# One-hot gate matrices in bf16, and the gate split into three bf16 parts

## The chip, the core and the metric

The program runs on one core of a Trainium2 chip. The metric is the device time of one execution in microseconds. The profile is one execution of the same program with the hardware profiler on; it names five engines: TensorE (PE for its matrix products, PEld for the weight loads ahead of them), VectorE (DVE), ScalarE (ACT), GpSimd (POOL) and the DMA queues issued by SyncE (SP).

## What is computed

The reference is a two-layer block (feed-forward, two kinds of attention), then a recurrent and an attention branch, and then a mixture of 16384 small experts (PEER). Only the last matters here. Each of the 256 tokens picks, for each of 8 heads, 16 experts out of 128 x 128 by two lists of 128 keys, and weighs them by a softmax:

```python
sc, ix = lax.top_k(s, PEER_TOPK)
cand = sc[:, :, 0, :, None] + sc[:, :, 1, None, :]
cidx = ix[:, :, 0, :, None] * PEER_N_KEYS + ix[:, :, 1, None, :]
top, pos = lax.top_k(cand.reshape(n, PEER_HEADS, PEER_TOPK * PEER_TOPK), PEER_TOPK)
eidx = jnp.take_along_axis(cidx.reshape(n, PEER_HEADS, -1), pos, axis=-1)
gate = jax.nn.softmax(top, axis=-1)
act = jax.nn.gelu(jnp.einsum('nhed,nd->nhe', expert_u[eidx], hb), approximate=False)
return jnp.einsum('nhe,nhed->nd', (gate * act).astype(hb.dtype), expert_v[eidx])
```

## The kernel before

The kernel does not gather experts. It computes the activation of all 16384 for all tokens, multiplies it by a gate that is zero for those that a token has not picked, and applies all of `expert_v`. An expert has two indices of 0 to 127; the first lies along the partitions, the second, i2, is the loop variable.

*u phases* (`u_phase`, 128 of them, one for each i2): 24 matrix products of 128 x 256 on TensorE, three for each of 8 slices, because fp32 weights are split in a high and a low fp32r part (`wblk`: a DMA brings 128 x 512 weights, ScalarE copies the high part, L200, and VectorE or GpSimd subtracts it for the low part, L206). ScalarE then writes the Gelu (L1299). Up to four such weight blocks are in flight.

*Scores and top-k* (`peer_scores`, `peer_topk`): ahead of them a norm (`norm`: for each of 8 slices ScalarE writes a high part L256 and a square L260, VectorE a low part L257) and the first queries, which ScalarE copies out as `qT`. Then a long chain on VectorE finds the picks. `res` holds, for each token, 128 picks (8 heads x 16): first index, second index, gate. While this runs, TensorE does the first 30 u phases.

*Gates* (`peer_gates`): `res` is transposed on TensorE so that the 128 picks lie along the partitions and the tokens along the row; five VectorE steps for each half of the tokens write them to `iT`: each index as a multiple of 8 and a remainder, and the gate.

*The stage of 64 gate groups* (`for tg in range(64)` in `peer`), four tokens each. For a token the gate matrix of 128 x 128 is a product over its 128 picks: a matrix with a one at each pick's first index, times a matrix with the gate at each pick's second index. `peer_hot` compares, for 16 tokens at a time, the multiple of 8 with 16 values and the remainder with 8 (L1441), and multiplies the gate into one of these (L1444). Every group then makes its two f32 matrices of 4 x 128 as products of a 16-wide and an 8-wide row (L1331, tiles `o0` and `o1`, two buffers each). TensorE multiplies them, one f32 product for each token (L1335, into a bank `pg`, two buffers). VectorE multiplies 30 columns of the result into activations that are already there (`ga0`, L1337), and ScalarE copies the other 98 to `ga1` (L1338). Between the groups lie 34 more u phases; all low parts L206 are VectorE's in this stage.

*v phases* (`v_phase`, L1355 to L1357) apply `expert_v`; in them the remaining 64 u phases. They reuse the tiles `o0` and `o1`. A linear stage (`ple`) ends the program.

A tile framework sets the order on each engine: it lists the instructions of every engine in a static order, found from the program's order and its own costs, and each engine then works its list strictly in that order, with semaphore waits between the engines.

Of the kernel before, what the change touches and what calls it, by code (L numbers as in the profile page):

```python
# [9 lines left out]
F32 = mybir.dt.float32  # L10
F32R = mybir.dt.float32r
I32 = mybir.dt.int32
U32 = mybir.dt.uint32
U16 = mybir.dt.uint16
BF16 = mybir.dt.bfloat16
AF = mybir.ActivationFunctionType
ALU = mybir.AluOpType
# [3 lines left out]
T = 256  # L21
# [1221 lines left out]
NKEY = 128  # L1243
# [24 lines left out]
class Prog3(Prog2):  # L1268
# [7 lines left out]
    def peer(self):  # L1276
        nc, tc, A = self.nc, self.tc, self.A
        E = ExitStack()
        with E:
            pp = E.enter_context(tc.tile_pool(name="pe", bufs=1))  # L1280
            C = {n: self.cload(pp, n) for n in ("ident", "iota")}
            ga0 = pp.tile([128, self.N0, T], F32, name="ga0")
            iT = pp.tile([128, 5, T], F32, name="iT")
            C["iota8"] = pp.tile([128, 16], F32, name="iota8")
            nc.vector.tensor_scalar(C["iota8"], C["iota"][:, 0:16], 8.0, None, op0=ALU.mult)
            ps = E.enter_context(tc.tile_pool(name="pps", bufs=2, space=PSUM))
            sp = E.enter_context(tc.tile_pool(name="psp", bufs=2))
            extra = {}

            def u_phase(i2):  # L1290
                if i2 < self.N0:
                    a = ga0[:, i2]
                elif self.N0 + self.NX <= i2 < self.N0 + self.NE:
                    a = extra[i2] = self.x[:, i2 - self.N0 - self.NX]
                else:
                    a = extra[i2] = sp.tile([128, T], F32, name="act", bufs=self.NX)
                p = ps.tile([128, 512], F32, name="pu")
                self.ws(p[:, :T], A["pu"][i2], self.xnh, self.xnl, KD)
                nc.scalar.activation(a, p[:, :T], AF.Gelu)  # L1299

            self.wsub = self.WS[0]
            tps = E.enter_context(tc.tile_pool(name="tps", bufs=2, space=PSUM))
            with tc.tile_pool(name="tk", bufs=1) as tk, tc.tile_pool(name="sps", bufs=4, space=PSUM) as sps:
                sc = self.peer_scores(tk, sps, ps)
                self.wsub = self.WS[1]
                res = tk.tile([128, 2, 3, HEADS_P, TOPK], F32, name="res")
                for t in range(2):
                    self.peer_topk(tk, sc[t], C, res[:, t])
                gates = self.peer_gates(tk, tps, res, iT, C)
                for i2 in range(self.N0):  # L1310
                    u_phase(i2)
                    if i2 in self.AT:
                        next(gates, None)
            ga1 = E.enter_context(tc.tile_pool(name="ga", bufs=1)).tile(
                [128, NKEY - self.N0, T], F32, name="ga1")
            xs = self.dram.tile([128, KD, T], F32, name="xp")
            nc.sync.dma_start(xs, self.x)
            self.wsub = self.WS[2]
            for tg in range(64):
                for i in range(tg * self.NE // 64, (tg + 1) * self.NE // 64):  # L1320
                    u_phase(self.N0 + i)
                pg = tps.tile([128, 4, NKEY], F32, name="pg")
                s = slice(tg * 4, tg * 4 + 4)
                if tg % 4 == 0:
                    hot = self.peer_hot(sp, iT, tg * 4, C)
                o = []
                for side in range(2):
                    o.append(sp.tile([128, 4, NKEY], F32, name=f"o{side}"))
                    u = slice(tg % 4 * 4, tg % 4 * 4 + 4)
                    B = [128, 4, 16, 8]  # L1330
                    nc.vector.tensor_mul(o[side].rearrange("p t (a b) -> p t a b", a=16),  # L1331
                                   hot[side][0][:, u, :, None].to_broadcast(B),
                                   hot[side][1][:, u, None, :].to_broadcast(B))
                for j in range(4):
                    nc.tensor.matmul(pg[:, j], o[0][:, j], o[1][:, j], start=True, stop=True)  # L1335
                a = ga0[:, :, s].rearrange("p i t -> p t i")
                nc.vector.tensor_mul(a, a, pg[:, :, :self.N0])  # L1337
                nc.scalar.activation(ga1[:, :, s].rearrange("p i t -> p t i"), pg[:, :, self.N0:], AF.Copy)  # L1338
            self.wsub = self.WS[3]
            vps = E.enter_context(tc.tile_pool(name="vps", bufs=1, space=PSUM))  # L1340
            acc = [vps.tile([128, 2, T], F32, name=f"acc{i}") for i in range(4)]

            def v_phase(i2, src):
                ph = sp.tile([128, 2 * T], F32R, name="o0")[:, 12:12 + T]
                pl = sp.tile([128, 2 * T], F32R, name="o1")[:, 12:12 + T]
                self.split(ph, pl, src)
                w = []
                for b in range(0, KD, self.wk):
                    w.append(self.wblk(A["pv"][i2][:, b * 128:(b + self.wk) * 128], self.wk * 128))
                for d in range(KD):  # L1350
                    o = acc[d // 2][:, d % 2]
                    vh, vl = w[d // self.wk]
                    s = slice(d % self.wk * 128, d % self.wk * 128 + 128)
                    first, last = i2 == 0 and d % 2 == 0, i2 == NKEY - 1
                    nc.tensor.matmul(o, vh[:, s], ph, start=first, stop=False, skip_group_check=True)  # L1355
                    nc.tensor.matmul(o, vh[:, s], pl, start=False, stop=False, skip_group_check=True)  # L1356
                    nc.tensor.matmul(o, vl[:, s], ph, start=False, stop=last, skip_group_check=True)  # L1357

            for i2 in range(NKEY):
                nx = i2 + self.N0 + self.NE  # L1360
                if i2 == NKEY // 2:
                    nc.sync.dma_start(self.x, xs)
                if nx < NKEY:
                    u_phase(nx)
                if i2 < self.N0:
                    v_phase(i2, ga0[:, i2])
                else:
                    g = ga1[:, i2 - self.N0]
                    nc.vector.tensor_mul(g, g, extra.pop(i2))
                    v_phase(i2, g)  # L1370
            self.wsub = "v"
            self.ple(sp, ps, tps, vps, acc)
# [55 lines left out]
        nc.vector.max(v[:, 8:16], tmp[:, :n])  # L1428
        nc.vector.max_index(i[:, 8:16], v[:, 8:16], tmp[:, :n])

    def peer_hot(self, sp, iT, t0, C):

        nc = self.nc
        s = slice(t0, t0 + 16)
        out = []
        for side in range(2):
            f = []
            for k, n in ((0, 16), (1, 8)):
                B = [128, 16, n]
                h = sp.tile(B, F32, name=f"h{side}{k}", bufs=1)  # L1440
                nc.vector.tensor_tensor(h, C["iota8" if k == 0 else "iota"][:, None, 0:n].to_broadcast(B),  # L1441
                                        iT[:, 2 * side + k, s, None].to_broadcast(B), op=ALU.is_equal)
                if side == 1 and k == 1:
                    nc.vector.tensor_mul(h, h, iT[:, 4, s, None].to_broadcast(B))  # L1444
                f.append(h)
            out.append(f)
        return out

    def peer_gates(self, tk, tps, res, iT, C):

        nc = self.nc
        B = [128, 2, HEADS_P, TOPK]
# [10 lines left out]
        for t in range(2):  # L1463
            pt = tps.tile([128, 4, NKEY], F32, name="pg")
            for j in range(3):
                nc.tensor.transpose(pt[:, j], res[:, t, j].rearrange("p h k -> p (h k)"), C["ident"])
            s = slice(t * 128, t * 128 + 128)
            ii = tk.tile([128, 2, NKEY], U32, name="ii")
            nc.vector.tensor_copy(ii, pt[:, 0:2])
            nc.vector.tensor_scalar(ii, ii, 7, None, op0=ALU.bitwise_and)  # L1470
            nc.vector.tensor_copy(iT[:, 1:4:2, s], ii)
            nc.vector.tensor_sub(iT[:, 0:4:2, s], pt[:, 0:2], iT[:, 1:4:2, s])
            nc.vector.tensor_copy(iT[:, 4, s], pt[:, 2])

    def peer_topk(self, tk, best, C, res):
        nc = self.nc
# [26 lines left out]
    def ple(self, sp, ps, tps, vps, acc):  # L1503

        nc, A = self.nc, self.A
# [6 lines left out]
        self.tmp, self.ps = Act, ps  # L1512
        pT = [Act.tile([128, T], F32, "p") for i in range(2)]
        ph = sp.tile([128, 2, T], F32R, name="o0")
        pl = sp.tile([128, 2, T], F32R, name="o1")
        for i in range(2):
            nc.sync.dma_start(pT[i], A["pT"][:, i])
            self.split(ph[:, i], pl[:, i], pT[i])
# [8 lines left out]
        for d in range(KD):  # L1527
            if d % 2 == 0:
                p = vps.tile([128, 2, T], F32, name=f"acc{d // 2}")
# [5 lines left out]
            s = Act.tile([128, T], F32, "s")  # L1535
# [56 lines left out]
```

## Time and profile before

| | us |
|---|---|
| three runs | 2194.35, 2195.75, 2196.25 |
| median | 2195.75 |
| the profiled execution | 2194.43 |
| its span, first to last instruction | 2192.6 |
| scores and top-k, about | 1300 to 1455 |
| the stage of 64 gate groups | 1460 to 1623 |
| v phases and the last stage | 1623 to 2192 |

The times of rows are microseconds from the start of the span. A row of the timeline has a start and a duration; instructions of an engine overlap, so what an engine can do in a stretch is read from start to start. Rows marked x3 or x16 are that many instructions in a row, and their duration runs from the first start to the last end.

### The profile page before, as it was taken

To read this page: it belongs to the slowest core of one execution; us is meant where nothing else is said; L and a number is where in the kernel's file an instruction comes from. 1 tells how busy PE (TensorE), PEld (TensorE's weight loads), DVE (VectorE), ACT (ScalarE), POOL (GpSimd) and SP (SyncE) were. 2 spreads that over 40 slices of the span, in tenths; PEclk is the share of its full clock that TensorE was granted. 3 is DMA by queue.
4 is the path that set the end of the run, shared out by engine and by line. 5 is a ranking of instruction groups with operands and counts; after the bars stand their busy time and mean duration, and the time that the engine had idled before them with its cause. 6 is when DMAs were issued, how large, how long until landed. Compare 5 with 4: busy or idle time off the path is not lost.

```text
span 2192.6 us, 48219 instructions
## 1 busy us (share of the span) xinstructions
PE 2092.4 (95%) x18034; PEld 2009.5 (92%) x18034; DVE 1602.2 (73%) x3315; ACT 1344.5 (61%) x2669; POOL 254.3 (12%) x250
## 2 busy tenths in 40 slices
PE   8999989999999999998897989889999999999997
PEld 8999779999999789998796789889999999999997
DVE  7766687767766677766995668999996666666666
ACT  6656676556656566657775656456665555555556
POOL 1001100000001100001210048950000000000000
PEclk9999999999999999999997999999999999999999
DMA  6666436666666336664353245543346666666663
GB/s 208 195 190 201 130 104 200 194 190 197 194 189 214 116 113 187 195 189 157 92 164 93 77 158 163 158 134 105 126 137 216 194 195 194 193 199 195 191 197 120
DMA packets 209659, 365.30 MB, mean 167 GB/s; under 512 B 31056, under 2 KB 39312, under 8 KB 208912
## 3 DMA queue, kind: packets, MB, share of 16 engines
q1 hardware_dynamic: 207312, 361.96, 54.7%
q8 instruction: 141, 2.31, 0.4%
q10 hardware_dynamic: 2112, 0.26, 0.1%
q14 instruction: 94, 0.77, 0.1%
HBM read 357.87 MB, written 4.26 MB: 165 GB/s over the span
## 4 chain that ended last, share of the span: by engine, by line
PE 75%; DVE 14%; ACT 4%; issue 4%; DMA 2%; POOL 1%; SPq 0%; DVEq 0%; ACTq 0%; POOLq 0%
PE mm L229 12%; PE mm L230 12%; PE mm L231 12%; PE acc L1357 5%; PE acc L1356 5%; PE acc L1355 5%; PE pu L230 4%; PE pu L229 4%; PE pu L231 4%; DVE wl L206 2%; PE pg L1335 2%; ACT wh L200 1%; DVE o L1331 1%; PE o L231 1%; PE o L229 1%
## 5 line engine op out<-in xcount | busy, mean ns | idle before, releaser
L200 ACT ACTIVATE wh<-wr 128x512 fp32r<-128x512 f32 (+1 forms) x1348 | 835.3, 624 | 618.7 <-PE mm L230 216.7
L206 DVE TENSOR_TENSOR wl<-wr,wh 128x512 fp32r<-128x512 f32 (+1 forms) x1256 | 866.6, 696 | 422.9 <-ACT wh L200 397.2
L229 PE MATMUL mm<-xn,wh 128*128 128x256 f32 x1840 | 512.4, 279 | 9.1 <-ACT wh L200 8.0
L231 PE MATMUL mm<-xn,wl 128*128 128x256 f32 x1840 | 509.8, 277 | 0.2 <-DVE wl L206 0.2
L230 PE MATMUL mm<-xn,wh 128*128 128x256 f32 x1840 | 509.9, 277 | 0.1
L229 PEld LDWEIGHTS mm<-xn,wh 128*128 128x128 f32 x1840 | 347.2, 189 | 12.0 <-ACT wh L200 9.5
L230 PEld LDWEIGHTS mm<-xn,wh 128*128 128x128 f32 x1840 | 347.2, 189 | 2.0 <-issue 1.2
L231 PEld LDWEIGHTS mm<-xn,wl 128*128 128x128 f32 x1840 | 346.9, 189 | 1.6 <-DVE wl L206 0.7
L231 PE MATMUL pu<-xn,wl 128*128 128x256 f32 x1024 | 283.8, 277 | 13.2 <-POOL wl L206 12.6
L229 PE MATMUL pu<-xn,wh 128*128 128x256 f32 x1024 | 285.9, 279 | 1.2 <-ACT ga L1299 1.2
L230 PE MATMUL pu<-xn,wh 128*128 128x256 f32 x1024 | 282.5, 276 | 0.0
L1355 PE MATMUL acc<-o,wh 128*128 128x256 f32 x1024 | 281.8, 275 | 0.6 <-ACT wh L200 0.6
L1357 PE MATMUL acc<-o,wl 128*128 128x256 f32 x1024 | 281.8, 275 | 0.2 <-DVE wl L206 0.2
L1356 PE MATMUL acc<-o,wh 128*128 128x256 f32 x1024 | 281.8, 275 | 0.0
L231 PEld LDWEIGHTS pu<-xn,wl 128*128 128x128 f32 x1024 | 192.4, 188 | 15.4 <-POOL wl L206 14.5
L229 PEld LDWEIGHTS pu<-xn,wh 128*128 128x128 f32 x1024 | 192.4, 188 | 1.4 <-ACT ga L1299 1.4
L231 PE MATMUL mm<-hh,wl 128*128 128x256 f32 x704 | 193.6, 275 | 0.0
L229 PE MATMUL mm<-hh,wh 128*128 128x256 f32 x704 | 193.6, 275 | 0.0
L230 PE MATMUL mm<-hh,wh 128*128 128x256 f32 x704 | 193.6, 275 | 0.0
L1355 PEld LDWEIGHTS acc<-o,wh 128*128 128x128 f32 x1024 | 192.3, 188 | 0.8 <-ACT wh L200 0.8
L1357 PEld LDWEIGHTS acc<-o,wl 128*128 128x128 f32 x1024 | 192.1, 188 | 0.4 <-DVE wl L206 0.4
L230 PEld LDWEIGHTS pu<-xn,wh 128*128 128x128 f32 x1024 | 192.4, 188 | 0.0
(444 smaller groups left out, 3741.0 us busy)
## 6 DMA issues: line engine op xcount, KB each, us to landing
wr<-in_ffn_gu SPq DMA_DIRECT2D x352, 256.0 KB, 3.0
wr<-in_pu SPq DMA_DIRECT2D x256, 256.0 KB, 2.9
wr<-in_pv SPq DMA_DIRECT2D x256, 256.0 KB, 2.9
wr<-in_ffn_d SPq DMA_DIRECT2D x160, 256.0 KB, 2.9
wr<-in_qk SPq DMA_DIRECT2D x64, 256.0 KB, 3.1
wr<-in_wo SPq DMA_DIRECT2D x48, 256.0 KB, 2.7
wr<-in_v SPq DMA_DIRECT2D x32, 256.0 KB, 2.9
wr<-in_u_g SPq DMA_DIRECT2D x32, 256.0 KB, 3.0
```

Of the source, the lines that this page charges most:

```text
L200: nc.scalar.activation(wh[:, :n], wr[:, :n], AF.Copy)
L206: (self.nc.gpsimd if eng == "p" else self.nc.vector).tensor_sub(out, a, b)
L229: self.nc.tensor.matmul(out, wh[:, s], h, start=first, stop=False, **kw)
L230: self.nc.tensor.matmul(out, wh[:, s], l, start=False, stop=False, **kw)
L231: self.nc.tensor.matmul(out, wl[:, s], h, start=False, stop=last, **kw)
L1331: nc.vector.tensor_mul(o[side].rearrange("p t (a b) -> p t a b", a=16), hot[side][0][:, u, :, None].to_broadcast(B), hot[side][1][:, u, No ...
L1335: nc.tensor.matmul(pg[:, j], o[0][:, j], o[1][:, j], start=True, stop=True)
L1355: nc.tensor.matmul(o, vh[:, s], ph, start=first, stop=False, skip_group_check=True)
L1356: nc.tensor.matmul(o, vh[:, s], pl, start=False, stop=False, skip_group_check=True)
L1357: nc.tensor.matmul(o, vl[:, s], ph, start=False, stop=last, skip_group_check=True)
```

## The change

The one-hot rows are no longer products of two short rows. An iota of 128 values, each repeated four times, is written in bf16 at the start (L1285, now a ScalarE copy; before, a VectorE step on 16 values). The two indices go to `iT` as they are, in bf16, which holds 0 to 127 exactly. The gate is written as three bf16 numbers whose sum is the fp32 gate: the gate in bf16, the rest in bf16, and the rest of that. A group then has two VectorE steps: one comparison of the iota with both indices of four tokens (L1325, 1024 elements), and one product of the second one-hot row with the three gate parts (L1328, 1536 elements). The four tokens of a group are innermost in these rows. TensorE does three bf16 products for each token, which add up in PSUM (L1332, 12 a group); it reads a token's columns four elements apart. Every bf16 product has a weight load of its own in the program. `peer_hot` is gone.

```diff
-            iT = pp.tile([128, 5, T], F32, name="iT")
-            C["iota8"] = pp.tile([128, 16], F32, name="iota8")
-            nc.vector.tensor_scalar(C["iota8"], C["iota"][:, 0:16], 8.0, None, op0=ALU.mult)
+            iT = pp.tile([128, 2, T], BF16, name="iT"), pp.tile([128, 3, T], BF16, name="gT")
+            C["iota4"] = pp.tile([128, NKEY + 8, 4], BF16, name="iota4")[:, :NKEY]
+            nc.scalar.activation(C["iota4"], C["iota"][:, :, None].to_broadcast([128, NKEY, 4]), AF.Copy)
...
-                if tg % 4 == 0:
-                    hot = self.peer_hot(sp, iT, tg * 4, C)
-                o = []
-                for side in range(2):
-                    o.append(sp.tile([128, 4, NKEY], F32, name=f"o{side}"))
-                    u = slice(tg % 4 * 4, tg % 4 * 4 + 4)
-                    B = [128, 4, 16, 8]
-                    nc.vector.tensor_mul(o[side].rearrange("p t (a b) -> p t a b", a=16),
-                                   hot[side][0][:, u, :, None].to_broadcast(B),
-                                   hot[side][1][:, u, None, :].to_broadcast(B))
+                one = sp.tile([128, 2, NKEY, 4], BF16, name="o0")
+                nc.vector.tensor_tensor(one, C["iota4"][:, None].to_broadcast([128, 2, NKEY, 4]),
+                                        iT[0][:, :, None, s].to_broadcast([128, 2, NKEY, 4]), op=ALU.is_equal)
+                og = sp.tile([128, 3, NKEY, 4], BF16, name="o1")
+                nc.vector.tensor_mul(og, one[:, 1:2].to_broadcast([128, 3, NKEY, 4]),
+                                     iT[1][:, :, None, s].to_broadcast([128, 3, NKEY, 4]))
                 for j in range(4):
-                    nc.tensor.matmul(pg[:, j], o[0][:, j], o[1][:, j], start=True, stop=True)
+                    for n in range(3):
+                        nc.tensor.matmul(pg[:, j], one[:, 0, :, j], og[:, n, :, j], start=n == 0, stop=n == 2)
...
-            ii = tk.tile([128, 2, NKEY], U32, name="ii")
-            nc.vector.tensor_copy(ii, pt[:, 0:2])
-            nc.vector.tensor_scalar(ii, ii, 7, None, op0=ALU.bitwise_and)
-            nc.vector.tensor_copy(iT[:, 1:4:2, s], ii)
-            nc.vector.tensor_sub(iT[:, 0:4:2, s], pt[:, 0:2], iT[:, 1:4:2, s])
-            nc.vector.tensor_copy(iT[:, 4, s], pt[:, 2])
+            nc.vector.tensor_copy(iT[0][:, :, s], pt[:, 0:2])
+            rest = tk.tile([128, NKEY], F32, name="rest")
+            nc.vector.tensor_copy(iT[1][:, 0, s], pt[:, 2])
+            nc.vector.tensor_sub(rest, pt[:, 2], iT[1][:, 0, s])
+            nc.vector.tensor_copy(iT[1][:, 1, s], rest)
+            nc.vector.tensor_sub(rest, rest, iT[1][:, 1, s])
+            nc.vector.tensor_copy(iT[1][:, 2, s], rest)
```

The change also makes the tile `o1` of the v phases and of the last stage half as large again, so that it has the size of the new matrix.

VectorE's list in the stage, a little after its start, before the change (`o` are the one-hot matrices, `h` the short rows, `ga` the scaling of activations, `wl` the low weight parts):

```order
L1331 TENSOR_TENSOR o_20225<-h_20218,h_20220 128x512
L1337 TENSOR_TENSOR ga_17787<-ga_17787,pg 128x4x30
L1331 TENSOR_TENSOR o_20273<-h_20214,h_20216 128x512
L1331 TENSOR_TENSOR o_20275<-h_20218,h_20220 128x512
L1337 TENSOR_TENSOR ga_17787<-ga_17787,pg 128x4x30
L1331 TENSOR_TENSOR o_20284<-h_20214,h_20216 128x512
L1331 TENSOR_TENSOR o_20286<-h_20218,h_20220 128x512
L206 TENSOR_TENSOR wl<-wr,wh 128x512 x3
L1337 TENSOR_TENSOR ga_17787<-ga_17787,pg 128x4x30
```

And the same list after it, at the same place (`iota` is the repeated iota, `gT` the gate parts):

```order
L1325 TENSOR_TENSOR o_20298<-iota_17790,iT 128x1024
L1334 TENSOR_TENSOR ga_17787<-ga_17787,pg 128x4x30
L1328 TENSOR_TENSOR o_20300<-o_20298,gT 128x1536
L1325 TENSOR_TENSOR o_20317<-iota_17790,iT 128x1024
L206 TENSOR_TENSOR wl<-wr,wh 128x512
L1328 TENSOR_TENSOR o_20319<-o_20317,gT 128x1536
L1334 TENSOR_TENSOR ga_17787<-ga_17787,pg 128x4x30
L1325 TENSOR_TENSOR o_20375<-iota_17790,iT 128x1024
L206 TENSOR_TENSOR wl<-wr,wh 128x512
L1334 TENSOR_TENSOR ga_17787<-ga_17787,pg 128x4x30
```

A group's two matrices L1331 have become L1325 and L1328, and the scaling (L1337, now L1334) still comes once a group, one or two matrices behind the one that it belongs to.

At the start of the expert part, VectorE's list of the norm loses the step that waits for the iota (`gh` are the norm's parts):

```order
 L324 TENSOR_TENSOR x<-k,o 128x256 x4
-L257 SCALAR_TENSOR_TENSOR gh<-x,vec,gh 128x256 x4
-L1285 TENSOR_SCALAR iota_17789<-c_iota 128x16
-L257 SCALAR_TENSOR_TENSOR gh<-x,vec,gh 128x256 x4
```

and ScalarE's list gains one, between its fourth and its fifth pair of the norm:

```order
 L256 ACTIVATE gh<-x,vec 128x256
 L260 ACTIVATE sq<-x 128x256
+L1285 ACTIVATE iota_17790<-c_iota 128x512
 L256 ACTIVATE gh<-x,vec 128x256
 L260 ACTIVATE sq<-x 128x256
```

So the wait for that DMA, which stood in the middle of VectorE's eight low parts, now stands in the middle of ScalarE's eight pairs.

## Rows read from the trace of the kernel before

**Rows 1.** The page, part 4: share of the span by engine.
```profile
PE 75%; DVE 14%; ACT 4%; issue 4%; DMA 2%; POOL 1%; SPq 0%; DVEq 0%; ACTq 0%; POOLq 0%
```

**Rows 2.** Busy time by windows: span, PE, PEld, DVE, ACT, POOL; clock, DMA share, GB/s.
```profile
1480.00:1600.00 120.00, 116.86 (x1003) 115.00 (x1002) 119.88 (x259) 75.62 (x126) 0.00 (x0) 1.00 0.35 114
...
sum 164.00, PE 159.05 PEld 156.14 DVE 161.41 ACT 102.54 POOL 0.00; mean PE 53.02 PEld 52.05 DVE 53.80 ACT 34.18 POOL 0.00
```

**Rows 3.** Groups by line, VectorE, 1455.5 to 1623: count, busy us, mean ns, idle before.
```profile
L1331 DVE TENSOR_TENSOR o<-h,h 128x512 f32<-128x512 f32 x128 | 83.2, 681 | 0.0
L206 DVE TENSOR_TENSOR wl<-wr,wh 128x512 fp32r<-128x512 f32 x72 | 46.4, 683 | 1.4 <-ACT wh L200 1.4
L1337 DVE TENSOR_TENSOR ga<-ga,pg 128x120 f32<-128x120 f32 x64 | 26.0, 406 | 0.3 <-PE pg L1335 0.2
L1441 DVE TENSOR_TENSOR h<-iota,iT 128x256 f32<-128x256 f32 x32 | 13.3, 415 | 0.0
L1441 DVE TENSOR_TENSOR h<-c_iota,iT 128x128 f32<-128x128 f32 x32 | 9.0, 282 | 0.0
L1444 DVE TENSOR_TENSOR h<-h,iT 128x128 f32<-128x128 f32 x16 | 4.5, 281 | 0.0
```

**Rows 4.** Timeline of VectorE in the stage: start us, duration us, instruction.
```profile
1499.97 0.41 DVE L1441 TENSOR_TENSOR h<-iota,iT 128x256 f32<-128x256 f32 x1
1500.31 0.28 DVE L1441 TENSOR_TENSOR h<-c_iota,iT 128x128 f32<-128x128 f32 x1
1500.51 0.41 DVE L1441 TENSOR_TENSOR h<-iota,iT 128x256 f32<-128x256 f32 x1
...
1501.85 0.40 DVE L1337 TENSOR_TENSOR ga<-ga,pg 128x120 f32<-128x120 f32 x1
1502.17 1.88 DVE L1331 TENSOR_TENSOR o<-h,h 128x512 f32<-128x512 f32 x3
```

**Rows 5.** Timeline of TensorE in the stage.
```profile
1502.59 0.28 PE L229 MATMUL pu<-xn,wh 128*128 128x256 f32 x1
...
1502.93 0.28 PE L229 MATMUL pu<-xn,wh 128*128 128x256 f32 x1
...
1503.84 1.87 PEld L1335 LDWEIGHTS pg<-o,o 128*128 128x128 f32 x16
```

**Rows 6.** Timeline of TensorE elsewhere: one-column products, and 64-column loads.
```profile
1249.62 1.15 PE L1211 MATMUL o<-k 128*64 128x64 f32 x32
...
1312.91 0.59 PE L276 MATMUL ps<-ones,sq 128*128 128x1 f32 x4
```

**Rows 7.** Timeline of VectorE from the gates to the last scaling.
```profile
1455.53 0.42 DVE L1469 CAST ii<-pg 128x256 uint32<-128x256 f32 x1 [0.42 <-PE pg L1466]
...
1458.97 0.28 DVE L1470 TENSOR_SCALAR ii<-ii 128x256 uint32<-128x256 uint32 x1
1459.17 0.28 DVE L1441 TENSOR_TENSOR h<-c_iota,iT 128x128 f32<-128x128 f32 x1
...
1460.64 0.68 DVE L1331 TENSOR_TENSOR o<-h,h 128x512 f32<-128x512 f32 x1
...
1622.40 0.42 DVE L1337 TENSOR_TENSOR ga<-ga,pg 128x120 f32<-128x120 f32 x1
```

**Rows 8.** Timeline of all engines in the norm ahead of the scores.
```profile
1300.90 0.42 SPq L170 DMA_DIRECT2D c_iota<-in_iota  x1
...
1303.30 0.49 ACT L256 ACTIVATE gh<-x,vec 128x256 fp32r<-128x256 f32 x1
...
1306.07 0.17 DVE L1285 TENSOR_SCALAR iota<-c_iota 128x16 f32<-128x16 f32 x1 [2.06 <-DMA c_iota<-in_iota]
...
1306.57 1.14 ACT L200 ACTIVATE wh<-wr 128x512 fp32r<-128x512 f32 x2
...
1310.40 0.66 ACT L1407 ACTIVATE qT<-pu 128x256 f32<-128x256 f32 x2 [2.70 <-PE pu L231]
```

More of the change, by code (lines that the diff above doesn't have):

```diff
@@ L1344, in v_phase @@
                 ph = sp.tile([128, 2 * T], F32R, name="o0")[:, 12:12 + T]
-                pl = sp.tile([128, 2 * T], F32R, name="o1")[:, 12:12 + T]
+                pl = sp.tile([128, 3 * T], F32R, name="o1")[:, 12:12 + T]
                 self.split(ph, pl, src)
@@ L1429, in top16 @@
         nc.vector.max_index(i[:, 8:16], v[:, 8:16], tmp[:, :n])
[L1431 to L1447, printed above, removed]
     def peer_gates(self, tk, tps, res, iT, C):
@@ L1514, in ple @@
         ph = sp.tile([128, 2, T], F32R, name="o0")
-        pl = sp.tile([128, 2, T], F32R, name="o1")
+        pl = sp.tile([128, 3, T], F32R, name="o1")
         for i in range(2):
```

## The prediction

> **What bounds the kernel now.** I read the page first: the chain that ended last is TensorE for 75% of the span [rows 1]. Outside one stage TensorE simply streams weights, and the change does not touch that. The stage it touches is the one in which u phases (24 products each) alternate with the 64 gate groups, so I cut the span there. In the 120 us from 1480 to 1600 TensorE shows 116.9 us busy and VectorE 119.9 us; in the whole stretch from 1460 to 1624 VectorE has 161.4 of 164 us [rows 2]. Both look full, so I counted each by starts. On VectorE, matrices of 512 elements follow one another every (1.88 - 0.68) / 2 = 0.60 us, those of 256 every 0.34, those of 128 every 0.20, and the scaling L1337 takes 0.32 from start to start [rows 4]: that is 0.07 us plus 1.04 ns for each element of a partition. On TensorE three u products take 1502.93 - 1502.59 = 0.34 us, 0.114 each, and the 16 halves of two gate groups follow one another every (1.87 - 0.19) / 15 = 0.112 us [rows 5].
>
> The sums by engine: VectorE, with the counts of [rows 3], 128 x 0.60 + 32 x 0.34 + 48 x 0.20 + 72 x 0.60 + 64 x 0.32 = 161.0 us, and 4.0 us for the ten small steps that turn the transposed gates into `iT` (1455.53 to 1460.64, less the four h matrices that lie among them), 165.0 in all. From the first of these steps to the end of the last L1337 there are 1622.40 + 0.32 - 1455.53 = 167.2 us [rows 7]. TensorE: 34 u phases x 24 x 0.114 = 93.0 and 512 x 0.112 = 57.3, 150 us. So VectorE bounds this stage with some 2 us of idle time, and TensorE has 11 us in hand. What comes after waits for the last L1337, and from there TensorE is the bound to the end; so what the stage gains or loses, the kernel gains or loses.
>
> **The gate matrices, on VectorE.** Out go the two 512-wide products of a group and the 20 h steps of every 16 tokens: 128 x 0.60 + 32 x 0.34 + 48 x 0.20 = 97.3 us. In come, for each of 64 groups, a comparison of 1024 bf16 elements (L1325) and a product of 1536 (L1328). No VectorE row here has bf16 on two sides. One end is one element at a time, as in [rows 4]: 0.07 + 1.04 x 1.024 = 1.13 and 0.07 + 1.04 x 1.536 = 1.67 us. The other end is cost by bytes: 1024 bf16 elements are the 2048 bytes of a 512-wide f32 matrix, 0.60 us, and 1536 are 0.07 + 1.04 x 0.768 = 0.87. A one-source step on 256 uint32 elements moved on after 0.20 us where two-source ones need 0.34 [rows 4, 7], so the engine can take two at a time in some form. I take the lower end: rows of four adjacent tokens leave every operand with neighbours innermost, which is what the layout is for. Then 64 x (0.60 + 0.87) = 94.1 us, a gain of 3.2. With the upper ends it would be 179.2, a loss of 82.
>
> The Trainium skill's page "VectorE: DVE Perf Modes", section "The perf-mode tier table", says that a two-source step on bf16 in SBUF runs at twice the fp32 rate; by it the sum is the same 94.1 us, and no run here shows it yet.
>
> **The splitting of the gate, on VectorE.** Ten steps at 4.0 us become twelve: two of 256 elements and ten of 128, 2 x 0.34 + 10 x 0.20 = 2.7 us, and some 0.1 us more at each of four places where a step needs the one ahead of it: 3.1. A gain of 0.9. These stand ahead of the first matrices, on the chain.
>
> **The gate products, on TensorE.** A group's 4 f32 products (8 halves, 0.90 us) become 12 bf16 ones, each with its own weight load. The trace has no bf16 product, so I bound a load with its product. A 128-column f32 load costs 0.113 us even if the product behind it has a single column ((0.59 - 0.25) / 3) [rows 6]: the load alone sets that pace. Loads of 64 f32 columns with 64-column products come every (1.15 - 0.22) / 31 = 0.030 us, two side by side, so 0.06 for one [rows 6]; a 128-column bf16 load has as many bytes. So a group costs between 12 x 0.06 = 0.72 and 12 x 0.112 = 1.34 us. With the lower end, to which I hold because both operands are half as wide, TensorE needs 93.0 + 46 = 139 us, well under VectorE, and the change of this term brings nothing: VectorE still ends last. The two engines meet where 93.0 + 768x = 157, at x = 0.083 us.
>
> Here a rule of the Trainium skill speaks against me and another for me. "TensorE: Matmul & The Clock Gate", section "LDWEIGHTS (loading the stationary operand)", gives a load as its columns over 1.2 GHz and names no type: 107 ns for 128 columns, an estimate by that page, which would make the stage as long as the first rival does. The f32 row of 0.113 agrees with it. The same page's section "Weight-path perf modes" says that loads of 128 columns that are not fp32 are read several elements at a time, which would give the lower end; no row here shows it.
>
> **What is queued where.** In VectorE's queue L1334, the scaling that waits for a group's products, stands right behind the next group's matrix, or one L206 behind it, as L1337 did. With 0.72 us for the products that wait is over before its turn, as now (0.3 us lost in the whole stage) [rows 3]. With 1.34 it is not, and L206 and the next matrices behind it wait too.
>
> **The iota, at the start of this part.** Before, VectorE waited 2.06 us at L1285 for the iota to land (issued 1300.90, there by 1306.07), and four low parts of the norm stood behind it [rows 8]. Now ScalarE waits there, after its fourth norm pair. Its fifth pair began at 1303.30; it will begin at 1306.07 plus 0.55 for a copy of 512 elements. Four pairs at (1306.57 - 1303.30) / 4 = 0.82 and the two weight copies (1.14) bring the two qT copies to 1306.62 + 3.28 + 1.14 = 1311.0 in place of 1310.40 [rows 8]. That is 0.6 us later, and VectorE's long top-k chain behind it starts as much later. Its ends: 0, if the iota lands sooner, and 3, if the two weight copies (3.3 us later than now) are waited for.
>
> **Sum.** -3.2 - 0.9 + 0.6, and -0.5 for VectorE's 1.4 us idle at the end of the stage, where TensorE, now lighter, was late [rows 3] (its ends 0 and -1.4): -4.0 us. The profiled execution took 2194.43 us and becomes 2190.4; the median of the runs shown is 2195.75, 1.3 higher, so I say **2191.8 us**. A kernel of this length tells no change from one under 0.2%, 4.4 us, which puts the edge at 2191.4: the forecast lies just inside "same". Its own range is 2188 to 2196, from 0.03 us on either bf16 step (64 x 0.06 = 3.8).
>
> **Rivals.**
> - *The weight load sets the pace of TensorE.* For it: the one-column row [rows 6]. Against it: half the bytes. Then a group's 12 products take 1.34 us, the stage's TensorE work is 93.0 + 768 x 0.112 = 179 us against the 161.8 us that this stretch has now (1460.64 to 1622.4) [rows 7], and VectorE stalls in L1334: slower by 17 to 21 us, 2213 to 2217. It decides from x = 0.083; from there to 0.1 it gives 2193 to 2207.
> - *VectorE takes the bf16 elements one at a time.* For it: every two-source row of the trace does [rows 4]; operands are repeated across the row with a step of nothing. Against it: the innermost run of four. Price 64 x (2.80 - 1.47) = 85 us, about 2277; if only the comparison falls back, 64 x 0.53 = 34, about 2226.
> - *The bf16 steps cost less than by bytes*, by 0.05 us or more each, or the idle time at both ends goes: 64 x 0.1 = 6 us more, about 2185. TensorE's 139 us leave room for it.
>
> **Chances.** Forecast 0.55, nearly half of it under the edge; full load pace 0.20 and the stretch between 0.10 (four parts in ten of it same); one at a time 0.10; cheaper steps 0.05. Faster by over 0.2%: 0.26 + 0.05 = 0.31. Same: 0.29 + 0.04 = 0.33. Slower: 0.20 + 0.06 + 0.10 = 0.36. The range, 2187 to 2217, takes in the load pace and leaves out the one-at-a-time rival, the end of the load pace and most of the cheap steps, under 0.2.
>
> **What will show it.** L1325 near 0.68 us and L1328 near 0.95 in their own durations (0.08 above start to start), against 1.2 and 1.75; the gate products' starts 0.06 apart, against 0.11; VectorE at over 97% of the stage with TensorE's share falling under 90%; no time lost ahead of L1334; ScalarE's 2.7 us wait at L1285 and qT copies at 1311. I am wrong if TensorE, not VectorE, is full from 1480 to 1600, or if a stage without gate work changes its length.

## The result and the profile after

The changed kernel takes 2214.8 us, the median of four runs (2212.5 to 2223.7), against 2195.05 for the four runs of the kernel before that are compared with it (2193.2 to 2196.3): 1.010 times the time, 95% interval 1.0086 to 1.0114. It is some 20 us slower. The profiled execution of the changed kernel took 2223.66 us, 9 over its median; a second trace of the same kernel, taken later, has a span of 2215.0 us, against 2192.6 before. The two agree in all that follows except where it is said.

The stage of 64 gate groups is where the time went. From the first gate step to the end of the last scaling it takes 1649.67 + 0.42 - 1456.13 = 194.0 us (192.6 in the second trace), where the same reckoning gives 167.3 before [rows 7]. What lies after the stage takes 571.7 us (569.5) in place of 569.8, and the stage begins 0.6 us later (2.6 us earlier) than before.

The page, part 4, the chain that ended last, by engine (before: [rows 1]):

```profile
PE 80%; DVE 10%; ACT 4%; issue 3%; DMA 2%; POOL 1%; SPq 0%; DVEq 0%; ACTq 0%; POOLq 0%
```

Busy time in the stage by windows: span, PE, PEld, DVE, ACT, POOL; clock, DMA share, GB/s (before: [rows 2]):

```profile
1480.00:1600.00 120.00, 120.00 (x1022) 117.43 (x1020) 102.22 (x166) 67.69 (x106) 0.00 (x0) 1.00 0.29 93
```

The two engines have changed places. TensorE is busy for all of the 120 us, with 1022 products: 0.117 us each. VectorE, which was the bound, is idle for 18 of them.

VectorE's groups by line in the whole stage (before: [rows 3]); the last number is the idle time ahead of them:

```profile
L1328 DVE TENSOR_TENSOR o<-o,gT 128x1536 bf16<-128x1536 bf16 x64 | 60.3, 952 | 0.0
L206 DVE TENSOR_TENSOR wl<-wr,wh 128x512 fp32r<-128x512 f32 x72 | 49.0, 685 | 1.6 <-ACT wh L200 1.4
L1325 DVE TENSOR_TENSOR o<-iota,iT 128x1024 bf16<-128x1024 bf16 x64 | 43.2, 685 | 0.0
L1334 DVE TENSOR_TENSOR ga<-ga,pg 128x120 f32<-128x120 f32 x64 | 26.7, 417 | 25.9 <-PE pg L1332 25.3
```

Nearly all of VectorE's 28 us of idle time stands in one place: 25.9 us ahead of the scaling L1334, 25.3 of it for the gate products. Before, the same step waited 0.3 us.

A piece of VectorE's timeline, and TensorE's gate products in the same 7 us (start, duration, instruction; the bracket is idle time and what ended it; before: [rows 4, 5]):

```profile
1518.61 0.68 DVE L1325 TENSOR_TENSOR o<-iota,iT 128x1024 bf16<-128x1024 bf16 x1
1519.83 0.42 DVE L1334 TENSOR_TENSOR ga<-ga,pg 128x120 f32<-128x120 f32 x1 [0.54 <-PE pg L1332]
1520.16 0.95 DVE L1328 TENSOR_TENSOR o<-o,gT 128x1536 bf16<-128x1536 bf16 x1
1521.03 0.69 DVE L1325 TENSOR_TENSOR o<-iota,iT 128x1024 bf16<-128x1024 bf16 x1
...
1516.67 1.58 PE L1332 MATMUL pg<-o,o 128*128 128x128 bf16 x12
1518.21 1.58 PE L1332 MATMUL pg<-o,o 128*128 128x128 bf16 x12
```

L1328 starts 1521.03 - 1520.16 = 0.87 us ahead of the next step, and L1334 0.33: VectorE's own prices are those of the forecast. But a group's twelve products take 1.58 us. Since one of them lasts 0.30, they start (1.58 - 0.30) / 11 = 0.116 apart, where the forecast had 0.06. The question for the runs was what holds a bf16 product of 128 columns at 0.117 us.

### The profile page after: what moved, and what is told of

It is laid out like the page before. It is cut to its first block, busy times and chain, and to the rows that moved or that the text cites. A ratio compares the mean times of both kernels' runs of the same rounds, so it can differ in the third digit from the quotient of the medians.

```text
span 2221.8 us, 48590 instructions
## 1 busy us (share of the span) xinstructions
PE 2127.2 (96%) x18290; PEld 2044.2 (92%) x18290; DVE 1604.7 (72%) x3236; ACT 1350.9 (61%) x2670; POOL 253.4 (11%) x250
## 4 chain that ended last, share of the span: by engine, by line
PE 80%; DVE 10%; ACT 4%; issue 3%; DMA 2%; POOL 1%; SPq 0%; DVEq 0%; ACTq 0%; POOLq 0%
PE mm L230 12%; PE mm L229 12%; PE mm L231 12%; PE acc L1354 5%; PE acc L1353 5%; PE acc L1352 5%; PE pu L229 5%; PE pu L230 5%; PE pu L231 5%; PE pg L1332 4%; DVE wl L206 1%; ACT wh L200 1%; PE o L231 1%; PE o L229 1%; PE o L230 1%
## 5 line engine op out<-in xcount | busy, mean ns | idle before, releaser
L200 ACT ACTIVATE wh<-wr 128x512 fp32r<-128x512 f32 (+1 forms) x1348 | 837.2, 625 | 636.4 <-PE mm L230 219.9
L229 PE MATMUL mm<-xn,wh 128*128 128x256 f32 x1840 | 512.6, 279 | 9.4 <-ACT wh L200 8.4
L229 PEld LDWEIGHTS mm<-xn,wh 128*128 128x128 f32 x1840 | 347.5, 189 | 12.1 <-ACT wh L200 9.8
L229 PE MATMUL pu<-xn,wh 128*128 128x256 f32 x1024 | 287.0, 280 | 0.7 <-ACT ga L1299 0.7
L229 PEld LDWEIGHTS pu<-xn,wh 128*128 128x128 f32 x1024 | 194.4, 190 | 1.0 <-ACT ga L1299 0.9
L229 PE MATMUL mm<-hh,wh 128*128 128x256 f32 x704 | 193.6, 275 | 0.0
```

The lines of the kernel that those rows point to most:

```text
L200: nc.scalar.activation(wh[:, :n], wr[:, :n], AF.Copy)
L229: self.nc.tensor.matmul(out, wh[:, s], h, start=first, stop=False, **kw)
```

## Experiments

All run times stand beside runs of the kernel before on the same chip: 2192.6 us (13 runs) for neighbouring columns on both sides, half of the moving columns, one product and one token innermost; 2194.2 (13 runs) for neighbouring columns on one side and two tokens innermost; 2193.5 (11 runs) for the place of the tiles. "Stage" is the time from the first gate step to the end of the last scaling.

### Neighbouring columns on both sides

```diff
-nc.tensor.matmul(pg[:, j], one[:, 0, :, j], og[:, n, :, j], ...)
+f = lambda x: x.rearrange("p k t -> p (k t)")[:, j * 128:j * 128 + 128]
+nc.tensor.matmul(pg[:, j], f(one[:, 0]), f(og[:, n]), ...)
```

> Each of the 768 gate products reads 128 neighbouring bf16 columns of the two matrices, for the weights and for the moving side, in place of columns four elements apart. Number and size of loads and products stay; the gate values are wrong, since the columns of four tokens are mixed. Theory A, the step of four elements in the rows makes load or product slow: starts of the products fall from 0.117 us to about 0.06, the stage is VectorE's again and the kernel takes about 2190 us. Theory B, a bf16 load of 128 columns costs what an f32 one does, whatever its layout: starts stay at 0.112 to 0.117, TensorE is full, and the time stays at 2210 to 2218 us.

Measured: 2186.4 us (one run), 0.056 us from product to product, a stage of 161.8 us. Since it mixes the columns of four tokens, this kernel is a probe and not one to use. Number, type and size of loads and products are unchanged, so neither the count of 768 loads nor "a load costs what it costs" explains the loss. The step of four elements does. With it gone, this run is 6 us under the median before, and the forecast's picture of the stage holds.

### Which side: weights or moving columns

One run gives only the weight loads neighbouring columns, another only the moving side.

```diff
+flat_weights: nc.tensor.matmul(pg[:, j], f(one[:, 0]), og[:, n, :, j], ...)
+flat_moving:  nc.tensor.matmul(pg[:, j], one[:, 0, :, j], f(og[:, n]), ...)
```

> Only the weight loads read 128 neighbouring columns; the moving side keeps its step of four elements. The gate values are wrong, since weights of four tokens are mixed. After the runs with both sides neighbouring (0.056 us from start to start, 2186.4 us) the step is the cause; this run and the next tell which side. Theory A1, the moving columns: starts stay at 0.117 us, TensorE stays full, 2210 to 2218 us. Theory A2, the weight columns: 0.056 us and about 2187 us.

> Only the moving side reads 128 neighbouring columns; the weight loads keep their step of four elements. The gate values are wrong in the same way. Theory A1, the moving columns: 0.056 us from start to start and about 2187 us; the run with 64 moving columns, 0.061 us, speaks for it. Theory A2, the weight columns: 0.117 us and 2210 to 2218 us.

A gate group on TensorE with neighbouring weights, from the timeline:

```profile
1502.81 1.55 PE L1332 MATMUL pg<-o,o 128*128 128x128 bf16 x12
```

And with neighbouring moving columns, with its twelve loads:

```profile
1501.11 0.86 PE L1332 MATMUL pg<-o,o 128*128 128x128 bf16 x12
...
1501.11 0.71 PEld L1332 LDWEIGHTS <-o 128*128 128x128 bf16 x12 [0.17 <-DVE o L1328]
```

With neighbouring weights alone, nothing is won: 2220.5 us (one run), stage 191.2. With neighbouring moving columns alone, all of it is: 2190.0 us (one run), stage 162.0, products (0.86 - 0.22) / 11 = 0.058 us apart, and the loads, still with their step of four elements, keep up. So it is the moving side. A 128-column bf16 load takes 0.058 us or less even with the step; a 128-column moving side with that step takes 0.117.

VectorE's and TensorE's busy time from 1480 to 1600 with neighbouring moving columns (columns as above):

```profile
1480.00:1600.00 120.00, 116.58 (x1237) 110.22 (x1234) 120.00 (x202) 81.67 (x130) 0.00 (x0) 1.00 0.36 114
```

VectorE is full again, and TensorE does 1237 products where it did 1022.

### Half of the moving columns

```diff
+h = 64 if n else 128
-nc.tensor.matmul(pg[:, j], one[:, 0, :, j], og[:, n, :, j], ...)
+nc.tensor.matmul(pg[:, j, :h], one[:, 0, :, j], og[:, n, :h, j], ...)
```

> The second and third product of each token move 64 columns in place of 128; loads as in the changed kernel. It leaves half of the columns of two gate parts out. Theory B, the load sets the pace: starts stay at 0.112 to 0.117 us and the time at 2210 to 2218. Theory C, the moving columns set it: 512 of the 768 products come after 0.06 us, TensorE's work falls by 512 x 0.057 = 29 us and the kernel takes about 2190 us.

A gate group on TensorE (the form in the row is that of its first product; eight of the twelve move 64 columns):

```profile
1501.93 1.15 PE L1333 MATMUL pg<-o,o 128*128 128x128 bf16 x12 [0.18 <-DVE o L1328]
```

The product behind one of 64 moving columns starts 0.060 to 0.063 us after it, the one behind one of 128 columns 0.119: the cost goes with the moving columns, 0.93 to 0.98 ns each at this step. Theory C was right on the product and wrong on the time: 2206.4 us (one run), stage 179.0. The mean of one product is here (0.119 + 2 x 0.062) / 3 = 0.081 us. The stage holds 36 u phases, as is told below, so TensorE's sum is 36 x 24 x 0.114 + 768 x 0.081 = 161 us. VectorE's is as much, 64 x (0.60 + 0.87 + 0.32) + 72 x 0.60 = 157.8 us and 3 for the splitting of the gate. But VectorE still lost 13.2 us ahead of the scaling (L1335 here), nearly all of it waiting for the products (L1333), and TensorE 5.0 waiting for the matrices:

```profile
L1335 DVE TENSOR_TENSOR ga<-ga,pg 128x120 f32<-128x120 f32 x64 | 26.8, 418 | 13.2 <-PE pg L1333 12.6
...
L1333 PE MATMUL pg<-o,o 128*128 128x64 bf16 (+1 forms) x768 | 72.6, 260 | 5.8 <-DVE o L1328 5.0 <-ACT wh L200 0.7
```

With about the same amount of work on both, handed over in a fixed order, neither engine was full in this run: each waited for the other in turn.

### One product in place of three

```diff
-for n in range(3):
+for n in range(1):
```

> VectorE's work is that of the changed kernel, but TensorE does only the first of the three products of a token: 256 loads and products in place of 768. It leaves the two smaller gate parts out of the sum. Whatever makes a product slow, TensorE then has 36 u phases x 24 x 0.114 + 256 x 0.117 = 128 us against VectorE's 161, so VectorE must bound the stage: the forecast for VectorE alone is 2190 to 2192 us, 4 us less than before, and L1334 waits for nothing. If the stage stays near 194 us, it was not the number of gate products that made it longer.

Measured: 2194.9 us (10 runs, 2187.9 to 2201.3), 1.0006 times before, interval 0.9993 to 1.002; stage 166.2 us. The number of products is thus what made the stage longer, but the 4 us that were expected beside it are not in the median. The trace is of a run of 2199.9 us. It is late already where the norm ahead of the scores begins, at 1303.3 us in place of 1300.5 before, and what comes after the stage takes 572.7 us in place of 569.8; the stage itself is 1.1 us shorter than before. In the stage the scaling waited 4.6 us for the products, and TensorE, idle for 16 of the 166 us, was not at its full clock throughout: the granted clock from 1560 to 1600 was 0.96 and 0.95, in the runs with neighbouring columns 1.00.

```profile
1560.00:1580.00 20.00, 17.04 (x124) 14.13 (x124) 18.68 (x32) 12.50 (x22) 0.00 (x0) 0.96 0.38 115
1580.00:1600.00 20.00, 18.69 (x139) 16.39 (x139) 18.95 (x33) 12.03 (x20) 0.00 (x0) 0.95 0.36 107
```

The two fastest of the ten runs, at 2187.9 us, have a mean granted clock of 0.990 over the span, the others 0.983 to 0.985. That the clock makes the spread is likely by this, not shown: there is one trace, and it is of one of the longest.

### One token innermost

The 128 keys stand innermost in the rows, so that TensorE reads neighbouring columns, and VectorE reads an index or a gate part as one value that is repeated along the row.

```diff
-one = sp.tile([128, 2, NKEY, 4], BF16, name="o0")
+one = sp.tile([128, 2, 4, NKEY], BF16, name="o0")
-iT[0][:, :, None, s].to_broadcast([128, 2, NKEY, 4])
+iT[0][:, :, s, None].to_broadcast([128, 2, 4, NKEY])
```

(and the same for `og`, with the iota no longer repeated)

> The same three bf16 products, with the 128 keys innermost in the rows in place of the four tokens; nothing is left out. TensorE reads neighbouring columns, and in both VectorE steps the index or gate part is one value repeated along the row. Theory A: starts near 0.06 us. Theory B: 0.112 to 0.117. On VectorE, if what made 1024 and 1536 elements cost 0.60 and 0.87 us is that the innermost run holds four different neighbours on every operand, they cost 1.13 and 1.67 now, VectorE has 64 x (1.13 + 1.67) + 64 = 243 us in the stage and the kernel takes about 2270 us. If a repeated value does no harm, VectorE is as in the changed kernel, and by A the time is about 2190 us, by B 2210 to 2218.

VectorE's groups by line between 1456 and 1650 (columns as above):

```profile
L1328 DVE TENSOR_TENSOR o<-o,gT 128x1536 bf16<-128x1536 bf16 x50 | 86.1, 1756 | 0.0
L1325 DVE TENSOR_TENSOR o<-iota,iT 128x1024 bf16<-128x1024 bf16 x50 | 59.4, 1221 | 0.0
```

From start to start they take 1.13 and 1.67 us, the one-element prices of the forecast's second rival. A piece of VectorE's timeline has one of each:

```profile
1518.58 1.22 DVE L1325 TENSOR_TENSOR o<-iota,iT 128x1024 bf16<-128x1024 bf16 x1
1519.72 0.69 DVE L206 TENSOR_TENSOR wl<-wr,wh 128x512 fp32r<-128x512 f32 x1
1520.32 1.76 DVE L1328 TENSOR_TENSOR o<-o,gT 128x1536 bf16<-128x1536 bf16 x1
1521.99 0.69 DVE L206 TENSOR_TENSOR wl<-wr,wh 128x512 fp32r<-128x512 f32 x1
```

TensorE's products are 0.056 us apart, and it doesn't help: 2294.5 us (two runs), stage 248.9. So the four tokens innermost are what lets VectorE take two bf16 elements at a time, and the same layout is what halves TensorE's moving side. The Trainium skill's page "Vector Engine (DVE) Microarchitecture Reference", section "Performance modes — why throughput varies by op and dtype", says that one element read over and over as an operand of a two-source bf16 step keeps the step at one result a cycle; the two steps above, at 1.13 and 1.67 us, agree.

### Two tokens innermost

```diff
-one = sp.tile([128, 2, NKEY, 4], BF16, name="o0")
+one = sp.tile([128, 4, NKEY, 2], BF16, name="o0")
-og = sp.tile([128, 3, NKEY, 4], BF16, name="o1")
+og = sp.tile([128, 2, 3, NKEY, 2], BF16, name="o1")
-nc.tensor.matmul(pg[:, j], one[:, 0, :, j], og[:, n, :, j], ...)
+nc.tensor.matmul(pg[:, j], one[:, j // 2 * 2, :, j % 2], og[:, j // 2, n, :, j % 2], ...)
```

(the indices and gate parts are stored pair by pair, so that VectorE still has one step for each matrix; the iota is repeated twice)

> Nothing is left out: two tokens innermost in the rows in place of four, so that TensorE's step is 4 bytes in place of 8. Theory P1, what costs is how many bytes lie from column to column, and 4 are as good as the f32r columns of the u products (0.114 us for 256 of them): 0.056 to 0.06 us, TensorE has room, and with VectorE as in the changed kernel (0.60 and 0.87 us) the time is that of the run with neighbouring columns, 2186 to 2190 us. Theory P2, any step over bf16 columns costs the double: 0.117 us, 2210 to 2218. On VectorE a run of two, if it does not count as neighbours, costs 1.13 and 1.67 us and the kernel about 2290 us, as the run with one token innermost did.

> Two tokens innermost and the gate as two bf16 parts in place of three, which leaves the third, smallest part out. VectorE's second step has 1024 elements, 0.60 us, so its stage has 64 x (0.60 + 0.60 + 0.32) + 72 x 0.60 = 140 us, some 17 less than with three parts; TensorE has 36 u phases x 24 x 0.114 = 98.5 and 512 x 0.056 = 29. By P1 the kernel takes 2168 to 2175 us, if TensorE is not held by anything else; by P2 TensorE has 98.5 + 512 x 0.117 = 158 us and the kernel about 2185.

Product and steps came out as P1 had them: gate products 0.057 us apart, VectorE's steps 0.60 and 0.87 from start to start. The stages took 163.2 us with three parts and 146.0 with two, the second against a sum of 140 for VectorE. A step of 4 bytes costs the moving side nothing, and a run of two is enough for VectorE. The totals did not: 2205.5 us (four runs, 1.0059 times before, interval 1.0038 to 1.0081) and 2192.4 (ten runs, 0.9995, interval 0.9983 to 1.0007). What comes after the stage took 589.2 and 588.8 us in place of 570, though nothing was changed there. In the list of tiles only one size had become odd: the iota of 544 bytes a partition, which is 8.5 times 64, and everything that is laid out behind it had moved by half of that 64, whole multiples aside.

### The place of the tiles

```diff
 C["iota4"] = pp.tile([128, NKEY + 8, 4], BF16, name="iota4")    # the change: 1088 bytes
+C["iota4"] = pp.tile([128, NKEY + 12, 4], BF16, name="iota4")   # after_shifted: 1120 bytes
+C["iota4"] = pp.tile([128, 2 * NKEY + 16, 2], BF16, name="iota4")  # pairs_padded, pairs_two_padded: 1088
```

> The changed kernel once more, for a second trace of it: the profiled execution of the first was 9 us over its median. TensorE full in the stage, starts 0.117 us apart, 191 to 194 us from the first gate step to the last scaling, as in the run with neighbouring weight columns (191.2); 2210 to 2218 us.

> The changed kernel with its repeated iota tile 32 bytes a partition longer (1120 in place of 1088 bytes), so that all tiles behind it lie 32 bytes further on; nothing else. In the run with two tokens innermost the iota was 544 bytes long, 32 short of a multiple of 64, its stage took 163.2 us as hoped, but what comes after it took 589.2 us in place of 568 to 572, with products of the v phases 0.117 and 0.124 us apart in place of 0.113. Theory S, the place of the v phases' tiles does that: 589 us after the stage here too, and 2230 to 2235 us in all. Theory L, it comes from the layout of the rows: 570 us, 2210 to 2218.

The v phases from 1800 to 2100, windows of the changed kernel and of the one with its tiles 32 bytes further on (columns as above):

```profile
1800.00:2100.00 300.00, 300.00 (x2649) 300.00 (x2648) 189.52 (x331) 171.93 (x331) 0.00 (x0) 1.00 0.66 195
```

```profile
1800.00:2100.00 300.00, 300.00 (x2555) 300.00 (x2554) 182.81 (x321) 165.99 (x319) 0.00 (x0) 1.00 0.61 188
```

The unshifted kernel, run again: 2217.2 us (two runs), stage 192.6, 569.5 after it, as expected. Shifted: 2239.3 us (two runs, 1.0204 times before, interval 1.0169 to 1.0239), stage 195.0, and 588.6 after it. In 300 us TensorE, full in both and at full clock, does 2649 products or 2555: 0.1133 or 0.1174 us each. Theory S holds. Of the total, 2239 against the 2230 to 2235 expected, part lies ahead of the stage (the gates begin 5 to 8 us later than in the two traces of the unshifted kernel, and 3.4 to 5.1 of this stand already at the start of the norm), which the v phases do not explain; and the 2239 is the middle of two runs 14 us apart. The run with one token innermost, with an iota of 272 bytes, also took 588.8 us after its stage, so that 19 of its 102 us are of this kind.

Which products slow down can be read from the traces. With two tokens innermost and the short iota, a u phase (first and last of its 24 products) and the v phase behind it:

```profile
1804.88 0.28 PE L229 MATMUL pu<-xn,wh 128*128 128x256 f32 x1
...
1807.48 0.28 PE L231 MATMUL pu<-xn,wl 128*128 128x256 f32 x1
1807.60 0.28 PE L1353 MATMUL acc<-o,wh 128*128 128x256 f32 x1
...
1810.35 0.28 PE L1355 MATMUL acc<-o,wl 128*128 128x256 f32 x1
```

The u products are 2.60 / 23 = 0.113 us apart, as ever, and the v products 2.75 / 23 = 0.120. So it is from 1800 to 2100 in all three runs with a short iota: 0.1133 and 0.120 in the mean. In the shifted run both lose, though not alike: u products are 0.1155 apart in the mean, v products 0.1187. So the place of the tiles does cost the 19 us, since the padding below takes them away again, but not every shift slows the same products. What in the place does it stays open.

> Two tokens innermost, three gate parts, nothing left out, and the iota padded to the 1088 bytes that it has in the changed kernel, so that the other tiles lie where they lay. Theory S: starts of the gate products 0.056 to 0.058 us, stage 162 to 163 us, 568 to 572 us after it, 2184 to 2190 us in all: 4 to 10 us under the kernel before and some 26 under the changed one. Theory L: 2205 as without the padding.

> The same with two gate parts, the third, smallest one left out. Its stage took 146.0 us without the padding. Theory S: 145 to 146 us for the stage and 568 to 572 after it, 2168 to 2176 us in all, about 20 us under the kernel before. Theory L: 2192 as without the padding.

With the padding, three parts take 2188.35 us (seven runs, 2185.8 to 2192.8): 0.9976 times before, interval 0.9963 to 0.9989. Stage 161.7, after it 570.2. Two parts take 2169.5 us (four runs, 2165.6 to 2170.8): 0.988 times before, interval 0.9863 to 0.9896; stage 146.7, after it 570.7. This is the fastest of all the kernels here; it leaves out the third gate part.

With three parts, two tokens innermost and the padding, TensorE and VectorE from 1480 to 1600, a gate group on TensorE, and VectorE's scaling over the stage:

```profile
1480.00:1600.00 120.00, 116.38 (x1240) 109.90 (x1239) 120.00 (x203) 81.34 (x129) 0.00 (x0) 1.00 0.36 113
...
1501.06 0.86 PE L1333 MATMUL pg<-o,o 128*128 128x128 bf16 x12
...
L1335 DVE TENSOR_TENSOR ga<-ga,pg 128x120 f32<-128x120 f32 x64 | 28.1, 439 | 0.0
```

That is the state which the forecast had described: VectorE full, a group's products over in 0.86 us, and no time lost ahead of the scaling.

## Why the prediction was wrong

**The step that failed is the term of the gate products on TensorE.** It was sized from weight loads alone: 0.06 us at the lower end and 0.112 at the upper one. Both ends were prices of loads, with rows in which the moving side is one column, or 64 neighbouring ones [rows 6]. The lower end was chosen "because both operands are half as wide". The text of the change said that TensorE reads a token's columns four elements apart, and the prediction used that layout only for VectorE. Measured: 0.117 us a product, 768 x 0.117 = 90 us in place of 46. The stage also holds 36 u phases, not the 34 that the prediction counted (the trace after has 290 products of L229 in it, the one before 291, eight to a phase), so TensorE's sum is 36 x 24 x 0.114 + 90 = 188 us, and it was full for all 194. With that the prediction's own sign of being wrong came true: TensorE, not VectorE, is full from 1480 to 1600. None of the rows that the prediction used has a moving side with a step, so the ends should have been kept and the forecast put nearer the upper one: beside the type, the step was what set the new product apart from those rows.

**The load was sized rightly.** With neighbouring moving columns the pair takes 0.056 to 0.058 us, which is the lower end. Of the two rules of the Trainium skill's page "TensorE: Matmul & The Clock Gate" that the prediction weighed, the one that reads bf16 loads of 128 columns several elements at a time agrees with this, and the one that gives a load its columns over 1.2 GHz and names no type does not.

**The first rival gave the right outcome by the wrong cause.** It said TensorE full at 0.112 us a product, VectorE waiting in L1334, 2213 to 2217 us; measured are 0.117, 25.3 us of waits in L1334, and 2214.8 us. It named the load as the cause, and the runs with either side alone showed the moving columns. Its sign, its place and the total were right, and it had a chance of 0.20. The total was partly luck: in the stage itself it expected a loss of 17 to 21 us, and the two traces lost 27 and 25.

**The matrices on VectorE** were right: 0.60 and 0.87 us from start to start. With TensorE's brake off, the stage took 161.7 to 162.0 us in three kernels, 5.5 us under the 167.3 of before; the forecast's terms for it (3.2, 0.9 and 0.5) make 4.6. The whole kernel came to 2186 to 2190 us there, against the 2191.8 of the forecast. The 0.5 us rested on a wait of VectorE at the end of the stage that was laid to TensorE; the row names ScalarE's L200 [rows 3]. In these three kernels that wait is 0.2 us or none at the end, but in two of them one of 1.1 to 1.2 us stands at the start.

**The second rival** fell for this kernel, and the run with one token innermost showed its prices to the hundredth, 1.13 and 1.67. The layout decided it, as the prediction had it.

**The iota** was a loss of 0.6 us in the sum. ScalarE's timeline in the norm (before: [rows 8]):

```profile
1299.69 0.51 ACT L256 ACTIVATE gh<-x,vec 128x256 fp32r<-128x256 f32 x1 [2.19 <-DVE x L324]
...
1303.72 0.63 ACT L1285 ACTIVATE iota<-c_iota 128x512 bf16<-128x512 f32 x1 [1.10 <-DMA c_iota<-in_iota]
...
1308.57 0.66 ACT L1404 ACTIVATE qT<-pu 128x256 f32<-128x256 f32 x2 [0.26 <-PE pu L231]
```

The wait is 1.10 us, not 2.7, since the DMA landed 3.5 us after its issue in place of 5.2; in the second trace it is 0.1. From the first norm part to the qT copies are 8.9 us (7.9 in the second trace), not the 9.9 of before: VectorE's low parts no longer stand behind the wait, and the copies no longer wait 2.7 us for the products that need them. So the copies came a microsecond or two earlier, where a loss was forecast. It did not reach the gates: from the first norm part to the first gate step are 156.4 us (154.9) against 155.1 before, since the stretch behind the copies took 147 us or more in both traces and 145.1 before. The prediction had let the chain behind the copies move with them. The term came to nothing that these traces can tell from zero.

**The point of balance.** The prediction let the two engines meet at 0.083 us a product, with no loss up to there. With 36 u phases and the splitting of the gate, the sums are 161 us on either engine at 0.081, so that the run with half of the moving columns stood at the balance itself. It took 2206.4 us, some 16 to 20 more than the runs with neighbouring moving columns. Most of this loss is thus in no sum of one engine: there each waits for the other. Where such waiting begins, between 0.058 and 0.081, no run shows.

## What to carry to other kernels

When an operand's layout is changed for one engine, price it on every engine that reads it, in the terms of that engine: here an innermost run of four made VectorE twice as fast and TensorE's moving side half as fast, and a run of two served both. A price from rows in which the new feature (a step, a type, an address) does not appear bounds nothing on that side; keep the far end as the forecast until a row or a run shows otherwise. When a tile is resized, look at what lies behind it: here an iota of 1088 bytes a partition (17 x 64) left the v phases as they were, and 1120, 544 and 272, none of them a multiple of 64, made them slower.

## What the runs showed of the chip

- TensorE's moving side, 128 bf16 columns at full clock: 0.056 to 0.058 us at a step of 2 or 4 bytes, 0.117 at 8 bytes; 64 columns at 8 bytes 0.060 to 0.063. Larger steps weren't tried. The Trainium skill's page "SBUF — State Buffer", section "Door 1: The DMA port swizzle (why `[64,N]` ≈ `[32,N]`)", says that two reads in each line of 16 bytes keep full bandwidth; at 8 bytes there are two, and the measurement is the double, so for this operand it does not hold.
- Weight loads do not mind the same step: with it, twelve bf16 loads of 128 columns took 0.71 us from the first start to the last end, in the run with neighbouring moving columns.
- VectorE takes two bf16 elements at a time on two sources if the innermost run holds two or four different neighbours (0.60 us for 1024 elements and 0.87 for 1536, from start to start), and one if an operand is one repeated value (1.13 and 1.67).
- A shift of the tiles by 32 bytes a partition raised TensorE's f32 products of 256 columns from 0.1133 to 0.1174 us in the mean, 19 us over the v phases and the last stage. With an iota of 544 or 272 bytes only the v products slowed, to 0.120 us. Why, and which other shifts do it, was not tried.
